# Table operands in PSUM, and all squares of x summed on TensorE, in an S5 block kernel

## The chip, the cores and the metric

One core of a Trainium2 chip runs the whole block; the other cores are idle. The metric is the device time of one execution in microseconds (us), over whole runs of the kernel. The core has five engines that run at the same time, each its own list of instructions in the order written: TensorE (PE in the rows; its loads of the stationary operand are PEld), VectorE (DVE), ScalarE (ACT), GpSimd (POOL), and SyncE (SP), which here only issues transfers. They wait for each other on semaphores. Matrix products and transposes are TensorE's and land in PSUM (8 banks of 512 numbers in each of 128 partitions); the rest of the data lies in SBUF.

## The reference

One layer of a diffusion block on 1024 latent tokens of width 1024, with 256 context tokens before them. Cut to what the change touches:

```python
mod = silu(c) @ ada_w + ada_b            # 6 x 1024; the context has its own, from c_ctx
xn  = modulate(rmsnorm(x, norm1_g), sh1, sc1)      # h * (1 + scale) + shift
cn  = modulate(rmsnorm(ctx, norm1_g), csh1, csc1)
for d in (forward, backward):            # S5: 64 groups of 16 channels, 64 complex states each
    lam_bar = exp(lam * dt);  k = (lam_bar - 1) / lam
    bb_re = k_re * b_re - k_im * b_im    # B_bar
    bb_im = k_re * b_im + k_im * b_re
    h_t = lam_bar * h_{t-1} + bb @ u_t   # context first, then the latent tokens
    y  += c_re @ h_re - c_im @ h_im
x = x + g1 * glu(gelu(y + d_skip * xn))
x = x + g2 * mlp(modulate(rmsnorm(x, norm2_g), sh2, sc2))     # 1024 -> 4096 -> 1024
out = rmsnorm(x, final_g)
```

All of it is float32.

## The kernel before

The program is written in issue order: each engine carries out its instructions in the order in which the Python text issues them, and no scheduler moves them. The tokens lie as 8 chunks `xu(j)`, 128 channels by 8 x 160 numbers (16 columns of context and 64 latent ones, for each of two halves). The scan is carried out in steps of 8 tokens: a table E of B_bar times powers of lam_bar turns 8 tokens at once into one state, so that TensorE can do it. The stages, in order of time:

- **Squares** (lines 148 to 154 and 171 to 197). ScalarE squares each chunk into one of four buffers (`sqt`, chosen by `sqb`), and TensorE sums over channels with a table `sel` into PSUM bank 1, eight matmuls a chunk. Of the first four chunks GpSimd adds 0 to 1 and 2 to 3 (L174, 128x1280), so that TensorE sums six buffers.
- **Discretisation** on VectorE (L158 to L207), then `b_bar` (L219 to L226) for groups 20 to 63 and later 0 to 19. ScalarE copies the powers into the tables `pt` (L193, L194) and, behind the last squares, `pg` (L209, L210). `transitions` (L256 to L261) fills tables that VectorE keeps in PSUM, and adds `pg[2]`.
- **Products of the tables** (`e_products`, L280 to L284): five instructions of 128x512 for each half chunk `(j, hlf)`, on VectorE for the five in `DVE_E`, on GpSimd for the other eleven. Both keep their inputs and the scratch operand `t` in SBUF. `turn_e` turns a half chunk with eight transposes and ScalarE copies the result (L296). Between them stand the scale of the tokens (L314 to L326) and the modulation: its matmuls (`cond1`, L301), the vector `md` (L429, L430), its spreading (L433) and ScalarE's copy `mu` (L437).
- **States and updates.** For every chunk j and group g `states` runs matmuls (L488 to L490) and two ScalarE copies (L491, L492). VectorE then runs `ups(j)`, five pieces of four instructions (L466 to L469) with their temporaries in PSUM; woven into its last piece is the context modulation `mod_ctx(j + 2)` (L450), two instructions of 128x256. `mod_ctx(0)` and `mod_ctx(1)` stand ahead of all updates. After chunks 5, 6 and 7 `k_finish` (L578 to L581) finishes a table of short kernels, which SyncE writes to memory in eight transfers (L584); on the same queue lie the writes of the modulated chunks (`save_u`, L453). GpSimd meanwhile makes the readout tables.
- **The scan** (L699 to L703) on VectorE, about 210 to 261 us, with five more `k_finish`; then readout, GLU gate and norm, and from about 475 us an MLP with a Strassen-like scheme (its matmuls are L772 to L774).

The lines that decide how the table products read their operands:

```python
eng, tm = (V, at(UT, 0, 5, 512)) if (j, hlf) in DVE_E else (P, sb(ETM, 5, 512))
er, ei, t = (vw(tm[:, i], 4, 16, 8) for i in (2 * hlf, 2 * hlf + 1, 4))
pr, pi, ps_ = (v[:, gs, None].to_broadcast(sh) for v in pt)
```

`at(UT, ...)` and `sb(...)` are SBUF, `bank(i)` and `PS` are PSUM; `vw` only gives a shape.

Of the kernel before, what the change touches and what calls it, by code (L numbers as in the profile page):

```python
# [10 lines left out]
OP = mybir.AluOpType  # L11
# [36 lines left out]
def kernel(ctx, tc, cst, bc, x, xl, ada_w, glu_w, w1, w2, out):  # L48
# [66 lines left out]
    ETM = 8192  # L115
# [26 lines left out]
    exb = C("ex")[:, None, :].to_broadcast([128, 64, NPOW])  # L142
    ssq = bank(1, 160)
    sqt = [at(E2[5], 0, 1280), at(E2[6], 0, 1280), at(E2[7], 0, 1280), at(X0, 2048, 1280)]
    sqb = (0, 1, 2, 3, 1, 3, 0, 2)

    def squares(j):
        S.activation(sqt[sqb[j]], xu(j, 1280), AF.Square)
# [19 lines left out]
    V.scalar_tensor_tensor(kk, ang, -1.0, ang, op0=OP.mult, op1=OP.max)  # L168
    S.activation(tb, ang, AF.Sin)
    S.activation(kk, kk, AF.Sin, scale=-1.0, bias=hpi)  # L170
    for j in (0, 2):
        squares(j)
        squares(j + 1)
        P.tensor_tensor(sqt[sqb[j]], sqt[sqb[j]], sqt[sqb[j + 1]], op=OP.add)  # L174
        sum_squares(j)
    V.tensor_scalar(sc, sc, 1.0, None, op0=OP.add)
    V.reciprocal(sc, sc)
# [17 lines left out]
    for j in range(4, 8):  # L195
        squares(j)
        sum_squares(j)

    V.tensor_scalar(q[0], pwr[:, :, 1], 1.0, None, op0=OP.subtract)
    V.tensor_tensor(q[3], pwi[:, :, 1], aim, op=OP.mult)  # L200
    V.tensor_tensor(q[2], q[0], are, op=OP.mult)
    V.tensor_tensor(q[4], pwi[:, :, 1], are, op=OP.mult)
    V.tensor_tensor(q[2], q[2], q[3], op=OP.add)
    V.tensor_tensor(q[3], q[0], aim, op=OP.mult)
    V.tensor_tensor(q[2], q[2], q[1], op=OP.mult)
    V.tensor_tensor(q[4], q[4], q[3], op=OP.subtract)
# [6 lines left out]
    def b_bar(a, b):  # L213

        gs = slice(a, b)
        n = b - a
        kre, kim = (q[i][:, gs, None].to_broadcast([128, n, 16]) for i in (2, 3))
        t1, t2 = (at(E2[4], 704 * i, n, 16) for i in range(2))
        V.tensor_tensor(t1, br[:, gs], kre, op=OP.mult)  # L219
        V.tensor_tensor(t2, bi[:, gs], kim, op=OP.mult)  # L220
        V.tensor_tensor(bd_[:, gs], bi[:, gs], kre, op=OP.mult)
        V.tensor_tensor(bi[:, gs], br[:, gs], kim, op=OP.mult)
        V.tensor_tensor(br[:, gs], t1, t2, op=OP.subtract)
        V.tensor_tensor(bi[:, gs], bi[:, gs], bd_[:, gs], op=OP.add)
# [27 lines left out]
    def transitions():  # L252

        for n in range(2):
            li = pwi[:, :, 8 + n]
            V.tensor_copy(LR[n], pwr[:, :, 8 + n])  # L256
            V.tensor_scalar(LI[n][:, :, 0], li, -1.0, None, op0=OP.mult)
            V.tensor_copy(LI[n][:, :, 1], li)
        V.tensor_copy(L32R, pwr[:, :, 10])
        V.tensor_copy(L32I, pwi[:, :, 10])  # L260
        V.tensor_tensor(pg[2], pg[0], pg[1], op=OP.add)  # L261

    def scan_transitions():
        l32 = L32.rearrange("p a g k c -> p (a g) k c")
# [65 lines left out]
    def dve_products(j, hlf):  # L330
        tp[j, hlf] = e_products(j, hlf)
# [1241 lines left out]
```

## Time and profile before

| | |
|---|---|
| time, median of 3 runs | 1100.47 us (1100.07 to 1103.93) |
| time of the profiled execution | 1100.8 us |
| its span, first to last instruction | 1099.0 us |
| mean granted clock of TensorE | 0.938 of full speed |
| busy: TensorE matmuls | 949.3 us (86%) |
| busy: VectorE | 915.3 us (83%) |
| busy: GpSimd | 610.4 us (56%) |
| busy: ScalarE | 551.3 us (50%) |
| chain that ended last | TensorE 46%, VectorE 31%, ScalarE 7%, issue 7%, DMA 4%, GpSimd 3% |

The chain is followed back from the last instruction to what released it, or to the instruction before it on its engine. Shares over the whole span mix stages with different limits, so a stage is read by its own window. In the rows, `out<-in` names the buffers: T and UT are the tables in SBUF, X the tokens and states, E the turned tables (and the buffers of the squares), GX a scratch tensor, PS is PSUM, KD and DX lie in memory. What stands in brackets at a row's end is the time that the engine was idle before the instruction, and the instruction that ended it. L12 is line 12 of the kernel before; in the orders below, of the changed kernel, lines of the later part are 4 to 11 higher.

### The profile page before, as it was taken

Reading aid. Unit: us, or ns where it says so; the run is one execution under the profiler, and the core shown is the slowest. Engines: PE = TensorE matmul, PEld = TensorE weight load, DVE = VectorE, ACT = ScalarE, POOL = GpSimd, SP = SyncE. Lnnn points to the kernel's source line nnn. Section 1 sums busy time; section 2 is a strip of 40 time slices with the busy share of each in tenths; the row PEclk is TensorE's granted clock in tenths of the full one; section 3 lists DMA queues with packets and bytes.
Section 4 is the critical chain, followed back from the end, with each engine's and each line's share of the span. In section 5 each row is a group of like instructions: output and inputs, shape, how many; then the busy total and the mean of one; then the engine's idle time right before and its main releaser. Section 6 shows DMA issues by size and latency. Waiting matters only on the chain.

```text
span 1099.0 us, 15197 instructions
## 1 busy us (share of the span) xinstructions
PE 949.3 (86%) x5244; PEld 779.7 (71%) x5244; DVE 915.3 (83%) x1393; ACT 551.3 (50%) x1012; POOL 610.4 (56%) x413
## 2 busy tenths in 40 slices
PE   3578675656799989789999999998889999999995
PEld 3347565535688867568888888886668888888875
DVE  8998999899993687789756565664899999999997
ACT  6238465334885446755655645453453434343413
POOL 3778899907373452354232324232788787778703
PEclk9779888776899999999999999999999999999998
DMA  9414355487576701145454444449453545351204
GB/s 385 181 31 147 118 163 139 96 220 202 164 234 210 254 20 38 68 158 191 162 175 139 157 149 156 161 139 339 165 190 131 174 135 164 123 193 39 77 1 154
DMA packets 104781, 168.85 MB, mean 154 GB/s; under 512 B 7680, under 2 KB 61952, under 8 KB 103424
## 3 DMA queue, kind: packets, MB, share of 16 engines
q1 hardware_dynamic: 100272, 153.20, 42.4%
q10 hardware_dynamic: 4432, 14.68, 4.1%
q8 instruction: 41, 0.67, 0.2%
q14 instruction: 36, 0.29, 0.1%
HBM read 120.40 MB, written 47.45 MB: 153 GB/s over the span
## 4 chain that ended last, share of the span: by engine, by line
PE 46%; DVE 31%; ACT 7%; issue 7%; DMA 4%; POOL 3%; SPq 1%; DVEq 0%; POOLq 0%; ACTq 0%
PE PS L774 14%; PE PS L773 14%; PE PS L772 14%; DVE T L1353 3%; DVE X L469 2%; DVE X L468 2%; DMA DY<-X 2%; DVE PS L467 2%; DVE PS L466 2%; DVE z L923 1%; DVE PS L699 1%; DVE W L923 1%; ACT T L724 1%; DVE X L450 1%; DVE UT L701 1%
## 5 line engine op out<-in xcount | busy, mean ns | idle before, releaser
L772 PE MATMUL PS<-z,W 128*128 128x512 f32 (+1 forms) x432 | 168.7, 390 | 2.9 <-DVE T L1173 1.5
L773 PE MATMUL PS<-z,W 128*128 128x512 f32 (+1 forms) x432 | 168.0, 389 | 2.4 <-DVE z L923 2.4
L774 PE MATMUL PS<-z,W 128*128 128x512 f32 (+1 forms) x404 | 156.9, 388 | 1.3 <-POOL W L923 1.2
L1353 DVE SCALAR_TENSOR_TENSOR T<-PS,T 128x512 f32<-128x512 f32 x160 | 112.1, 739 | 2.4 <-PE PS L774 2.2
L773 PE MATMUL PS<-W 128*128 128x512 f32 (+1 forms) x244 | 94.5, 387 | 4.7 <-DVE W L923 4.7
L772 PEld LDWEIGHTS PS<-z,W 128*128 128x128 f32 x432 | 81.8, 189 | 20.7 <-DVE T L1452 2.2
L773 PEld LDWEIGHTS PS<-z,W 128*128 128x128 f32 x432 | 81.8, 189 | 19.9 <-DVE z L923 3.7
L772 PE MATMUL PS<-W 128*128 128x512 f32 (+1 forms) x244 | 93.9, 385 | 0.0
L774 PEld LDWEIGHTS PS<-z,W 128*128 128x128 f32 x404 | 76.6, 190 | 18.1 <-POOL W L923 2.1
L923 DVE TENSOR_TENSOR z<-z 128x512 fp32r<-128x512 f32 x60 | 81.2, 1378 | 6.0 <-ACT z L926 6.0
L774 PE MATMUL PS<-W 128*128 128x512 f32 (+1 forms) x216 | 83.4, 386 | 1.5 <-POOL W L923 1.5
L774 PE MATMUL PS<-z,A 128*128 128x512 f32 x208 | 81.3, 391 | 2.5 <-POOL A L923 2.5
L923 DVE TENSOR_TENSOR W<-W 128x512 fp32r<-128x512 f32 x49 | 74.1, 1535 | 7.2 <-ACT W L926 7.2
L1201 POOL TENSOR_TENSOR T<-T 128x512 f32<-128x512 f32 x27 | 39.2, 1455 | 68.2 <-ACT T L1144 60.0
L488 PE MATMUL PS<-X,E 128*64 128x160 f32 x256 | 50.4, 337 | 29.0 <-DVE X L450 17.1
L774 PE MATMUL PS<-W,A 128*128 128x512 f32 x184 | 71.7, 390 | 0.3 <-POOL A L923 0.3
L772 PE MATMUL PS<-z,A 128*128 128x512 f32 x180 | 70.2, 390 | 0.0
L1173 DVE TENSOR_TENSOR T<-T,PS 128x512 f32<-128x512 f32 x64 | 42.9, 684 | 32.7 <-PE PS L774 32.0
L773 PE MATMUL PS<-z,A 128*128 128x512 f32 x180 | 70.0, 389 | 0.0
L926 ACT CAST W<-T 128x512 fp32r<-128x512 f32 (+1 forms) x46 | 33.0, 718 | 65.1 <-POOL T L1272 42.5
L926 ACT CAST W<-UT 128x512 fp32r<-128x512 f32 (+2 forms) x50 | 35.6, 713 | 58.6 <-POOL UT L1272 37.8
L488 PEld LDWEIGHTS PS<-X,E 128*64 128x64 f32 x256 | 34.8, 152 | 40.2 <-issue 22.9
(329 smaller groups left out, 2780.8 us busy)
## 6 DMA issues: line engine op xcount, KB each, us to landing
YD<-T SPq DMA_DIRECT2D x88, 256.0 KB, 2.3
z<-YD SPq DMA_DIRECT2D x60, 256.0 KB, 3.8
W<-YD SPq DMA_DIRECT2D x49, 256.0 KB, 4.1
T<-in_w_dram SPq DMA_DIRECT2D x9, 1024.0 KB, 5.8
T<-in_ada_w_dram ACTq DMA_DIRECT2D x17, 512.0 KB, 4.1
UT<-in_w_dram SPq DMA_DIRECT2D x8, 1024.0 KB, 5.8
T<-in_w_dram SPq DMA_DIRECT2D x20, 384.0 KB, 3.4
UT<-in_w_dram SPq DMA_DIRECT2D x15, 384.0 KB, 4.4
```

The costliest lines, as they stand in the source:

```text
L466: ops = [lambda: eng.tensor_tensor(ta, src, lr, op=OP.mult), lambda: eng.tensor_tensor(tb_, src[:, :, ::-1], li, op=OP.mult), lambda: eng. ...
L467: lambda: eng.tensor_tensor(tb_, src[:, :, ::-1], li, op=OP.mult),
L468: lambda: eng.tensor_tensor(out_, out_, ta, op=OP.add),
L488: PE.matmul(b[0:64, c], e[:, g, c, 0:64], uj[:, g], start=True, stop=True)
L772: PE.matmul(o, wt[0], xt[0], start=start, stop=False)
L773: PE.matmul(o, wt[0], xt[1], start=False, stop=False)
L774: PE.matmul(o, wt[1], xt[0], start=False, stop=stop)
L923: eng.tensor_tensor(lo, src, hi.bitcast(F32), op=OP.subtract)
L926: S.copy(vw(to[0][:, 0:size(dims)], *dims) if dims else to[0], src)
L1173: V.tensor_tensor(to, x_, o, op=OP.add)
L1201: P.tensor_tensor(o, x_, z_, op=op)
L1353: V.scalar_tensor_tensor(o, src, g2[:, d:d + 1], o, op0=OP.mult, op1=OP.add)
```

## The change

It has five parts.

1. ScalarE's squares of all eight chunks go to TensorE one by one; GpSimd's two adds are gone, and the square buffers rotate in plain order.
2. Powers of the first 20 groups (`pt[0]` and `pt[1]`, all that VectorE's products need) are copied to PSUM bank 1 (`ptv`, two ScalarE copies), behind the sums of squares that lie in the same bank. VectorE's products read them there and keep their scratch `t` in PSUM too.
3. The factors k of the discretisation (`hold`) and two temporaries of `b_bar` (`t2`, `t3`) lie in PSUM.
4. The sum `pg[2]` moves from ahead of VectorE's first product to behind its third.
5. The context's modulation of chunks 2 to 7 is copied to PSUM (`muc`, one ScalarE copy) and read there by `mod_ctx`; `k_finish` on VectorE keeps the two values `dj` and `ks` in PSUM.

```diff
-    sqb = (0, 1, 2, 3, 1, 3, 0, 2)
+    sqb = (0, 1, 2, 3, 0, 1, 2, 3)
...
-    for j in (0, 2):
+    for j in range(4):
         squares(j)
-        squares(j + 1)
-        P.tensor_tensor(sqt[sqb[j]], sqt[sqb[j]], sqt[sqb[j + 1]], op=OP.add)
         sum_squares(j)
...
+    ptv = [vw(bank(1, 160, 160 + 160 * i), 20, 8) for i in range(2)]
+    for i in range(2):
+        S.copy(ptv[i], pt[i][:, 0:20])
+
+    hold = [PS[:, 3616 + 64 * i:3680 + 64 * i] for i in range(2)]
...
-    V.tensor_tensor(q[2], q[2], q[1], op=OP.mult)
+    V.tensor_tensor(hold[0], q[2], q[1], op=OP.mult)
     V.tensor_tensor(q[4], q[4], q[3], op=OP.subtract)
-    V.tensor_tensor(q[3], q[4], q[1], op=OP.mult)
+    V.tensor_tensor(hold[1], q[4], q[1], op=OP.mult)
...
-        t1, t2 = (at(E2[4], 704 * i, n, 16) for i in range(2))
+        kre, kim = (h[:, gs, None].to_broadcast([128, n, 16]) for h in hold)
+        t1, t2, t3 = at(E2[4], 0, n, 16), *(vw(PS[:, o:o + 16 * n], n, 16) for o in (1024, 2048))
         V.tensor_tensor(t1, br[:, gs], kre, op=OP.mult)
         V.tensor_tensor(t2, bi[:, gs], kim, op=OP.mult)
-        V.tensor_tensor(bd_[:, gs], bi[:, gs], kre, op=OP.mult)
+        V.tensor_tensor(t3, bi[:, gs], kre, op=OP.mult)
...
-        V.tensor_tensor(bi[:, gs], bi[:, gs], bd_[:, gs], op=OP.add)
+        V.tensor_tensor(bi[:, gs], bi[:, gs], t3, op=OP.add)
...
-        V.tensor_tensor(pg[2], pg[0], pg[1], op=OP.add)
...
-        er, ei, t = (vw(tm[:, i], 4, 16, 8) for i in (2 * hlf, 2 * hlf + 1, 4))
+        er, ei = (vw(tm[:, i], 4, 16, 8) for i in (2 * hlf, 2 * hlf + 1))
+        t = vw(PS[:, 2976:3488] if on_v else tm[:, 4], 4, 16, 8)
...
-        pr, pi, ps_ = (v[:, gs, None].to_broadcast(sh) for v in pt)
+        pr, pi, ps_ = (v[:, gs, None].to_broadcast(sh) for v in (*(ptv if on_v else pt[:2]), pt[2]))
...
     dve_products(1, 0)
+    V.tensor_tensor(pg[2], pg[0], pg[1], op=OP.add)
...
+    muc = vw(PS[:, 3488:3584], 8, 2, 6)
     S.copy(mu, vw(bank(6, 256), 8, 2, 8, 2))
+    S.copy(muc, mu[:, :, :, 2:8, 1])
...
-        sc_, sh_ = (mu[:, :, i, j, 1:2][:, :, :, None].to_broadcast([128, 8, 2, 16]) for i in (1, 0))
+        sc_, sh_ = ((mu[:, :, i, j, 1:2] if j < 2 else muc[:, :, i, j - 2:j - 1])[:, :, :, None].to_broadcast([128, 8, 2, 16]) for i in (1, 0))
...
+            dj, ks = (vw(PS[r:r + 16, o:o + 128], 8, 16) for o in (3200, 3328))
...
-        eng.tensor_tensor(kf, kf, dj, op=OP.add)
-        eng.tensor_tensor(k0, k0, kf, op=OP.add)
+        eng.tensor_tensor(ks, kf, dj, op=OP.add)
+        eng.tensor_tensor(k0, k0, ks, op=OP.add)
```

ScalarE before, from the fifth square (L148) over the four `pg` copies (L209, L210) to the root for the token scale (L315):

```order
L148 ACTIVATE E_6_76<-X_69 128x1280 [waits DMAHW6_49,Pool_49]
L148 ACTIVATE X_68<-X_69 128x1280 [waits DMAHW7_49,Pool_49]
L148 ACTIVATE E_5_75<-X_69 128x1280 [waits DMAHW0_49,PE_49]
L148 ACTIVATE E_7_77<-X_69 128x1280 [waits DMAHW1_49,PE_49]
L209 COPY T<-E_2_72 64x512
L210 COPY T<-E_2_72 64x512
L209 COPY T<-UT 64x512
L210 COPY T<-UT 64x512
L315 ACT_TABLE_LOAD
L315 ACTIVATE GX<-GX 128x160 [waits DVE_49]
```

The same stretch now (the `pg` copies are L212 and L213, the root is L319):

```order
L148 ACTIVATE E_5_75<-X_69 128x1280 [waits DMAHW6_49,PE_49,Activation_49]
L148 ACTIVATE E_6_76<-X_69 128x1280 [waits DMAHW7_49,PE_49,Activation_49]
L148 ACTIVATE E_7_77<-X_69 128x1280 [waits DMAHW0_49,PE_49,Activation_49]
L148 ACTIVATE X_68<-X_69 128x1280 [waits DMAHW1_49,PE_49,Activation_49]
L199 COPY PS<-T 128x160 [waits PE_49,Activation_49]
L199 COPY PS<-T 128x160 [waits Activation_49]
L212 COPY T<-E_2_72 64x512
L213 COPY T<-E_2_72 64x512
L212 COPY T<-UT 64x512
L213 COPY T<-UT 64x512
L319 ACT_TABLE_LOAD
L319 ACTIVATE GX<-GX 128x160 [waits DVE_49]
```

Two copies from T to PSUM (L199) stand between the last square and the `pg` copies, and the first of them waits for TensorE.

VectorE before, from the last table copy to PSUM (L260) over the sum `pg[2]` (L261) and the products of (0,0) (L280 to L284) to the first row of the token scale:

```order
L260 COPY PS<-UT 128x64 [waits DVE_49]
L261 TENSOR_TENSOR T<-T 128x512 [waits Activation_49]
L280 TENSOR_TENSOR UT<-T 128x512 [waits DVE_49,Pool_49]
L281 TENSOR_TENSOR UT<-T 128x512
L282 TENSOR_TENSOR UT<-UT 128x512 [waits DVE_49]
L283 TENSOR_TENSOR UT<-T 128x512 [waits DVE_49]
L284 TENSOR_TENSOR UT<-UT 128x512 [waits DVE_49]
L314 TENSOR_SCALAR GX<-PS 128x160 [waits PE_49]
```

The same place now (products L284 to L288):

```order
L263 COPY PS<-UT 128x64 [waits DVE_49]
L284 TENSOR_TENSOR UT<-T 128x512 [waits DVE_49,Activation_49,Pool_49]
L285 TENSOR_TENSOR PS<-PS,T 128x512 [waits PE_49]
L286 TENSOR_TENSOR UT<-UT,PS 128x512 [waits DVE_49]
L287 TENSOR_TENSOR PS<-PS,T 128x512 [waits DVE_49]
L288 TENSOR_TENSOR UT<-UT,PS 128x512 [waits DVE_49]
L318 TENSOR_SCALAR GX<-PS 128x160
```

The sum is gone from here, the first product also waits for ScalarE, the second for TensorE, and four of the five have a PSUM input.

VectorE before, the products of (2,0) and the first context modulation (L450):

```order
L280 TENSOR_TENSOR UT<-T 128x512
L281 TENSOR_TENSOR UT<-T 128x512
L282 TENSOR_TENSOR UT<-UT 128x512 [waits DVE_49]
L283 TENSOR_TENSOR UT<-T 128x512 [waits DVE_49]
L284 TENSOR_TENSOR UT<-UT 128x512 [waits DVE_49]
L450 TENSOR_TENSOR X_69<-X_69,T 128x16x16 [waits Activation_49]
```

The same place now, from the product's first row:

```order
L284 TENSOR_TENSOR UT<-T 128x512
L285 TENSOR_TENSOR PS<-PS,T 128x512 [waits DVE_49,PE_49,Activation_49]
L286 TENSOR_TENSOR UT<-UT,PS 128x512 [waits DVE_49]
L287 TENSOR_TENSOR PS<-PS,T 128x512 [waits DVE_49]
L288 TENSOR_TENSOR UT<-UT,PS 128x512 [waits DVE_49]
L457 TENSOR_TENSOR X_69<-X_69,T 128x16x16
```

The second product has taken over the wait for ScalarE, and waits for TensorE as well.

## Rows read from the trace of the kernel before

**Rows 1.** VectorE's waits, 0 to 261 us: us in total, times, longest us.
```profile
DVE PS L466 <- ACT X L491: 4.1, 2, 2.1
DVE T L429 <- PE PS L424: 0.7, 1, 0.7
```

**Rows 2.** Timeline of GpSimd and VectorE: start us, us, then the instruction.
```profile
15.14 2.95 POOL L174 TENSOR_TENSOR E<-E,E 128x1280 f32<-128x1280 f32 x1 [10.40 <-ACT E L148]
15.24 2.94 DVE L200 TENSOR_TENSOR UT<-UT,T 128x64 f32<-128x64 f32 x1
```

**Rows 3.** VectorE's timeline, 69 and 262 us; updates by shape (busy us, mean ns).
```profile
69.04 0.68 DVE L280 TENSOR_TENSOR UT<-T 128x512 f32<-128x512 f32 x1
L466 DVE TENSOR_TENSOR PS<-X,PS 128x528 f32<-128x528 f32 x24 | 17.0, 710 | 5.0 <-ACT X L491 4.1
262.61 0.69 DVE L466 TENSOR_TENSOR UT<-X,PS 128x512 f32<-128x512 f32 x1
```

**Rows 4.** TensorE's timeline, sums: matmuls, then weight loads (18 to 19.5 us).
```profile
18.15 9.46 PE L154 MATMUL PS<-E,T 128*128 128x160 f32 x48 [18.15 <-POOL E L174]
29.61 4.51 PE L154 MATMUL PS<-E,T 128*128 128x160 f32 x32
18.15 1.57 PEld L154 LDWEIGHTS PS<-E,T 128*128 128x128 f32 x6 [18.15 <-POOL E L174]
```

**Rows 5.** ScalarE's timeline: the first three squares, the first `pg` copy.
```profile
12.65 3.57 ACT L148 ACTIVATE E<-X 128x1280 f32<-128x1280 f32 x3
26.65 0.62 ACT L209 COPY T<-E 64x512 f32<-64x512 f32 x1
```

**Rows 6.** VectorE's timeline: where products (0,0), (1,0), (2,0) begin and end.
```profile
42.19 1.74 DVE L280 TENSOR_TENSOR UT<-T 128x512 f32<-128x512 f32 x1
49.94 0.31 DVE L314 TENSOR_SCALAR GX<-PS 128x160 f32<-128x160 f32 x1
58.45 1.59 DVE L280 TENSOR_TENSOR UT<-T 128x512 f32<-128x512 f32 x1
66.24 2.87 DVE L326 TENSOR_TENSOR X<-X,PS 128x1280 f32<-128x1280 f32 x2
76.32 1.53 DVE L280 TENSOR_TENSOR UT<-T 128x512 f32<-128x512 f32 x1
81.61 1.62 DVE L450 TENSOR_TENSOR X<-X,T 128x256 f32<-128x256 f32 x2
```

**Rows 7.** Timelines of ScalarE and VectorE: modulation copy, VectorE's second update.
```profile
80.01 0.38 ACT L437 COPY T<-PS 128x256 f32<-128x256 f32 x1 [2.67 <-PE PS L433]
94.56 0.71 DVE L466 TENSOR_TENSOR PS<-X,PS 128x528 f32<-128x528 f32 x1 [2.01 <-ACT X L491]
```

**Rows 8.** VectorE: context modulation by shape; a 128x256 update on the timeline.
```profile
L450 DVE TENSOR_TENSOR X<-X,T 128x256 f32<-128x256 f32 x16 | 17.2, 1076 | 0.1
275.12 0.41 DVE L466 TENSOR_TENSOR UT<-X,PS 128x256 f32<-128x256 f32 x1
```

**Rows 9.** Timelines of VectorE and ScalarE: `k_finish` and what stands around it.
```profile
175.12 1.24 DVE L578 TENSOR_TENSOR T<-T 16x128 f32<-16x128 f32 x1
178.88 0.71 DVE L466 TENSOR_TENSOR PS<-X,PS 128x528 f32<-128x528 f32 x1
207.02 0.67 DVE L578 TENSOR_TENSOR T<-T 16x128 f32<-16x128 f32 x1
210.10 0.28 DVE L265 COPY PS<-PS 128x128 f32<-128x128 f32 x1
228.04 0.28 DVE L580 TENSOR_TENSOR T<-T 16x128 f32<-16x128 f32 x1
189.71 0.38 ACT L491 COPY X<-PS 128x264 f32<-128x264 f32 x1 [10.98 <-DMA DX<-X]
197.53 0.71 DVE L466 TENSOR_TENSOR PS<-X,PS 128x528 f32<-128x528 f32 x1 [2.07 <-ACT X L491]
```

**Rows 10.** Windows: us, each engine's busy us (count), PEclk, DMA share, GB/s.
```profile
475.00:1089.00 614.00, 596.56 (x2654) 489.50 (x2652) 501.14 (x640) 281.47 (x454) 327.50 (x189) 1.00 0.45 150
```

More of the change, by code (lines that the diff above doesn't have):

```diff
@@ L216, in b_bar @@
         n = b - a
-        kre, kim = (q[i][:, gs, None].to_broadcast([128, n, 16]) for i in (2, 3))
-        t1, t2 = (at(E2[4], 704 * i, n, 16) for i in range(2))
+        kre, kim = (h[:, gs, None].to_broadcast([128, n, 16]) for h in hold)
+        t1, t2, t3 = at(E2[4], 0, n, 16), *(vw(PS[:, o:o + 16 * n], n, 16) for o in (1024, 2048))
         V.tensor_tensor(t1, br[:, gs], kre, op=OP.mult)
         V.tensor_tensor(t2, bi[:, gs], kim, op=OP.mult)
-        V.tensor_tensor(bd_[:, gs], bi[:, gs], kre, op=OP.mult)
+        V.tensor_tensor(t3, bi[:, gs], kre, op=OP.mult)
         V.tensor_tensor(bi[:, gs], br[:, gs], kim, op=OP.mult)
         V.tensor_tensor(br[:, gs], t1, t2, op=OP.subtract)
-        V.tensor_tensor(bi[:, gs], bi[:, gs], bd_[:, gs], op=OP.add)
+        V.tensor_tensor(bi[:, gs], bi[:, gs], t3, op=OP.add)
         V.tensor_tensor(bs[:, gs], br[:, gs], bi[:, gs], op=OP.add)
@@ L272, in e_products @@
     def e_products(j, hlf):
-        eng, tm = (V, at(UT, 0, 5, 512)) if (j, hlf) in DVE_E else (P, sb(ETM, 5, 512))
-        er, ei, t = (vw(tm[:, i], 4, 16, 8) for i in (2 * hlf, 2 * hlf + 1, 4))
+        on_v = (j, hlf) in DVE_E
+        eng, tm = (V, at(UT, 0, 4, 512)) if on_v else (P, sb(ETM, 5, 512))
+        er, ei = (vw(tm[:, i], 4, 16, 8) for i in (2 * hlf, 2 * hlf + 1))
+        t = vw(PS[:, 2976:3488] if on_v else tm[:, 4], 4, 16, 8)
         gs = slice(8 * j + 4 * hlf, 8 * j + 4 * hlf + 4)
         sh = [128, 4, 16, 8]
-        pr, pi, ps_ = (v[:, gs, None].to_broadcast(sh) for v in pt)
+        pr, pi, ps_ = (v[:, gs, None].to_broadcast(sh) for v in (*(ptv if on_v else pt[:2]), pt[2]))
         b, d, s = (v[:, gs, :, None].to_broadcast(sh) for v in (br, bd_, bs))
@@ L577, in k_finish @@
         k0, kf, dj = ksr(j, 0, 8, 15, 16)[:, :, 7], ksr(j, 1920, 8, 16), ksr(j, 2048, 8, 16)
+        ks = kf
+        if eng is V:
+            r = 32 + 64 * (j % 2)
+            dj, ks = (vw(PS[r:r + 16, o:o + 128], 8, 16) for o in (3200, 3328))
         eng.tensor_tensor(dj, ident[32:48, None, 32:48].to_broadcast([16, 8, 16]),
                         C("dg")[32:48, 8 * j:8 * j + 8, None].to_broadcast([16, 8, 16]), op=OP.mult)
-        eng.tensor_tensor(kf, kf, dj, op=OP.add)
-        eng.tensor_tensor(k0, k0, kf, op=OP.add)
+        eng.tensor_tensor(ks, kf, dj, op=OP.add)
+        eng.tensor_tensor(k0, k0, ks, op=OP.add)
         kd = KD[j].rearrange("(h t g c) -> t h g c", h=16, t=8, g=8)
```

## The prediction

> **What bounds the kernel now.** I read the page's busy slices first, then the chain of work that ended last, then VectorE's waits up to the scan's end, the timeline of the four engines that the change touches, and the windows by stage.
>
> VectorE's waits over the first 261 us are short: ScalarE's copies of the states hold it 4.1 us, TensorE 0.7 us [rows 1]. Up to the end of the scan VectorE is therefore the spine of the program, and every microsecond taken from its instructions, or from something it comes to wait for, moves all that follows. After it come the readout, the gate and the MLP, which the change does not touch, and which should slide as a block; the MLP's 614 us are TensorE's, 596.6 us busy at a granted clock of 1.00 [rows 10].
>
> Why VectorE is slow in places is seen in two stretches. While GpSimd runs its 128x1280 add for 2.95 us, a VectorE product of 64 elements a row takes 2.94 us: it starts 0.1 us later and ends together with it [rows 2]. The instructions of the table products, 128x512 with both inputs in SBUF, take 0.68 us where GpSimd is idle [rows 3] and 1.5 to 1.7 us where it runs its own products [rows 6]. The update instruction with one input in PSUM is not held: 24 of 128x528 average 710 ns though GpSimd works through most of that stage [rows 3]. So the reading is that an instruction with two SBUF inputs waits for the GpSimd instruction in progress, and one with a PSUM input does not.
>
> **The change, part by part.** The sum is made against the profiled execution, 1100.8 us (span 1099.0), which is 0.3 us above the median of the three runs.
>
> *The gate of the first product.* Part (0,0) starts at 42.19 us now [rows 6]. Without GpSimd's two adds VectorE loses two holds of nearly 3 us each, without the sum `pg[2]` 0.6 us, and so could be there at about 36.1; the PSUM temporaries of `b_bar` make it earlier still (its last eight instructions run beside GpSimd). But the first product now waits for ScalarE's last `pg` copy, these stand behind the two new table copies, and those wait for the last sum of squares. That sum is longer: 64 matmuls instead of 48, of two records each. The 96 records now run from 18.15 to 34.12 us, 2.4 us more than 96 at the later pace of 0.141 us (4.51 us for 32), because the first ones ran at 0.26 (1.57 us for six) [rows 4]. With the first square done at 13.9 [rows 5] I take 13.95 + 128 x 0.141 + 2.4 = 34.4 for the last sum. All at the fast pace it is 32.0, all at the slow pace 47.2. Two table copies of 128x160, priced at no more than ScalarE's 0.38 us for 128x256 [rows 7], and four `pg` copies of 0.62 [rows 5], with the hand-overs, give a start at **38.0: 4.2 us gained**. All else gained before that point goes into VectorE's new wait. Behind it on VectorE stands everything; GpSimd's own products, which take no part in that wait, start earlier.
>
> *The five products.* Two of the five instructions of each keep two SBUF inputs only in the first (`ei`); four get a PSUM input. One held instruction at 1.35 us (between 0.6 and 1.7) and four at 0.7 us give 4.1. Now (0,0) takes 7.75 us, (1,0) 7.79, (2,0) 5.29, and (1,1), undisturbed, 5 x 0.68 = 3.4 [rows 3, 6]. That gains 3.65 in (0,0) and 3.7 in (1,0), and loses 0.5 in (1,1), if GpSimd is then at work; (0,1), held in its first instruction alone, stays as it is. The moved `pg[2]` sum costs up to 1.3 where it now stands (0.64 alone, more beside GpSimd). VectorE's 0.7 us wait for the modulation's transposes goes [rows 1], since TensorE's chain there was itself late by (1,0). In (2,0) the second instruction now waits for the modulation matmuls and two ScalarE copies, because its PSUM bank is one that TensorE's sums of modulation fill: about 0.6 lost in all. With the gate this is 4.2 + 3.65 + 3.7 - 0.5 - 1.3 + 0.7 - 0.6 = 9.85 us at the first context modulation (81.6 now [rows 6]).
>
> VectorE then waits 2.01 us at its second update for ScalarE's state copies [rows 7]. These hang on the modulation copy at 80.01, whose matmuls come earlier by 10.45 (all of that but the last 0.6) and no longer stand behind a pair of transposes; the new 128x96 copy takes back under 0.38. The update should resume 11.2 us earlier, between VectorE's 9.85 and some 11.6 of the copies. **First part: 11.2** (bounds 7 to 14).
>
> *Context modulation.* Sixteen instructions of 128x256 with two SBUF inputs average 1.076 us; twelve of them, for chunks 2 to 7, get a PSUM input. VectorE's 128x256 with one PSUM input takes 0.41 us [rows 8]. 12 x (1.076 - 0.41) = **8.0 us**, all on VectorE, in the stage where it hardly waits. The lower bound is nothing, if the state copies cannot come faster.
>
> *Finishing the short kernels.* `k_finish(0)` takes from 175.12 to 178.88, `k_finish(2)` from 207.02 to 210.10, each three instructions of 128 elements; undisturbed ones in the scan take 0.28 [rows 9]. The first still has two SBUF inputs and stays, the other two get a PSUM input: 1.24 + 2 x 0.28 = 1.8, and 0.67 + 0.56 = 1.2. Gain 2.0 + 1.9 = **3.8 us** (0 to 4.5). `k_finish(1)` is given nothing, since VectorE waits 2.07 us for ScalarE soon behind it [rows 9]: ScalarE's copies before that stand 10.98 us for a saved chunk, which lies on SyncE's queue behind the eight writes of `k_finish(0)`. Those in the scan gain nothing either.
>
> *Free edits.* The factors `hold` in PSUM and `b_bar`'s temporaries lie ahead of the gate, under VectorE's new wait; without the gate they would be worth some 4 us more. SyncE's and GpSimd's queues carry the same transfers in the same order.
>
> Sum: 11.2 + 8.0 + 3.8 = 23.0; 1100.8 - 23.0 = **1077.8, forecast 1078 us**.
>
> [...] An update writing a 128x512 buffer in SBUF from one SBUF and one PSUM input takes 0.69 us, the same work from two SBUF inputs 0.68 [rows 3]: moving an operand costs an undisturbed instruction 0.01 us at most, and the sum counts nothing. [...]
>
> **The rivals.**
>
> *TensorE stays slow through the sums.* Then the last sum ends at 47.2 and the gate opens 12.8 us later: 1077.8 + 12.8 = **1090.6**. For it: the first records ran at 0.26 [rows 4]. Against: the rest ran at 0.141 without a break, and the new sums are denser. Chance 0.08.
>
> *The state copies bound the updates.* VectorE gets through its modulation sooner and waits for ScalarE or TensorE as long: 1077.8 + 8.0 = **1085.8**. For it: two waits of 2 us there now [rows 1]. Against: there are no others of that size in that stage. Chance 0.12.
>
> *The change does not do what it says:* an instruction with one SBUF input is held by GpSimd all the same. Products, modulation and `k_finish` stay as they are, and the gate's 4.2 with the lost wait of 0.7, less 1.3 for `pg[2]`, is all: 1100.8 - 3.6 = **1097**. Against: the 710 ns of 24 updates [rows 3]. Chance 0.03.
>
> [...] Chance 0.05. [...]
>
> *Slower: TensorE gets a lower clock in the MLP.* The 614 us there ran at 1.00 [rows 10]; a kernel that reaches them sooner, with other pauses before, may get less. Each 0.01 costs some 6 us, so 0.04 eats the gain and below about 0.954 the kernel is slower by over 0.5%: 1077.8 + 614 x 0.05 = **1108**. Nothing in the trace speaks for it beyond the clock having been below 1.00 in earlier stages. Chance 0.03.
>
> **How the numbers follow.** The forecast has 0.69, the rivals 0.08, 0.12, 0.03, 0.05 and 0.03. The forecast's own bounds (first part 7 to 14, `k_finish` 0 to 4.5) give 1074 to 1086 around 1078; taking in the second and fourth rival and leaving out the others the range is **1073 to 1088**. About 0.5%, 5.5 us, is what a measurement of this kernel tells from no change. Faster by more than that: all but the third and the last, 0.93 (with a share for surprises taken off); same 0.04, slower 0.03.
>
> **What would show it.** In the changed kernel: GpSimd free of the 128x1280 adds, and VectorE's products of 64 elements back at about 0.2 us; VectorE waiting some 4 to 8 us for ScalarE before the first product, which starts near 38; four of five product instructions at 0.7 us beside a busy GpSimd; twelve modulations near 0.41; the scan starting near 187 instead of 210; the MLP at clock 1.00 over 614 us. The forecast is wrong if the first product starts after 42, if VectorE's waits for ScalarE between 80 and 190 grow by more than 5 us, or if the stage after the scan grows, because its loads from memory come no sooner.

## The result

The changed kernel takes 1075.3 us at the median of 4 runs (1074.2 to 1078.0), against 1102.2 us (1100.1 to 1105.6) for the kernel before in the same comparison: a ratio of 0.9757, 95% interval 0.9737 to 0.9777. In a second comparison it took 1076.2 against 1102.6 us, 0.9768 (0.9743 to 0.9792). The forecast was 1078, range 1073 to 1088. The two profiled executions stand 26.0 us apart, with spans of 1099.0 and 1073.0 us.

| | before | after |
|---|---|---|
| profiled execution, us | 1100.8 | 1074.8 |
| span, us | 1099.0 | 1073.0 |
| mean granted clock of TensorE | 0.938 | 0.944 |
| busy: TensorE matmuls, us | 949.3 | 954.5 |
| busy: VectorE, us | 915.3 | 884.0 |
| busy: GpSimd, us | 610.4 | 599.7 |
| busy: ScalarE, us | 551.3 | 552.9 |

VectorE lost 31.3 us of busy time and TensorE gained 5.2, of which 4.2 are in the sums that GpSimd no longer shortens. VectorE's waits up to 261 us, which before were those of [rows 1], one of 0.5 us, and one of 4.0 us at the very start (now 3.8), are now these (us in total, times, longest us):

```profile
DVE UT L284 <- ACT T L213: 5.6, 1, 5.6
DVE PS L473 <- ACT X L498: 3.8, 2, 2.7
...
DVE PS L285 <- ACT PS L444: 1.4, 1, 1.4
```

The first and the last are the two waits that the change puts in, in the places where the prediction had them. The first is the gate of the first product. TensorE's timeline and ScalarE's show what it hangs on: the last sum ends at 31.41 + 2.34 = 33.75 us, and the two table copies (L199) and four `pg` copies (L212, L213) follow at once.

```profile
13.79 9.09 PE L154 MATMUL PS<-E,T 128*128 128x160 f32 x48 [13.79 <-ACT E L148]
...
24.89 6.68 PE L154 MATMUL PS<-E,T 128*128 128x160 f32 x48
31.41 2.34 PE L154 MATMUL PS<-X,T 128*128 128x160 f32 x16
```

```profile
33.84 0.62 ACT L199 COPY PS<-T 128x160 f32<-128x160 f32 x2 [7.43 <-PE PS L154]
34.40 0.64 ACT L212 COPY T<-E 64x512 f32<-64x512 f32 x1
...
36.38 0.67 ACT L213 COPY T<-UT 64x512 f32<-64x512 f32 x1
```

VectorE's timeline from the gate on, with the two waits, the first context modulation and the second update:

```profile
15.07 0.26 DVE L203 TENSOR_TENSOR UT<-UT,T 128x64 f32<-128x64 f32 x1
...
37.13 1.17 DVE L284 TENSOR_TENSOR UT<-T 128x512 f32<-128x512 f32 x1 [5.61 <-ACT T L213]
38.22 0.69 DVE L285 TENSOR_TENSOR PS<-PS,T 128x512 f32<-128x512 f32 x1
...
68.43 0.70 DVE L285 TENSOR_TENSOR PS<-PS,T 128x512 f32<-128x512 f32 x1 [1.42 <-ACT PS L444]
...
71.23 2.08 DVE L457 TENSOR_TENSOR X<-X,T 128x256 f32<-128x256 f32 x2
...
83.99 0.71 DVE L473 TENSOR_TENSOR PS<-X,PS 128x528 f32<-128x528 f32 x1 [1.11 <-ACT X L498]
```

The row at 15.07 is the 64-element product that took 2.94 us beside GpSimd's add [rows 2] and now takes 0.26. The product (0,0) begins at 37.13 and is over in 3.9 us instead of 7.75 [rows 6]: its first instruction, still with two SBUF inputs, takes 1.17 us, the second, which reads PSUM, 0.69. The modulation of 128x256 by shape (busy us, mean ns) stands at 0.41 us, the price of [rows 8]:

```profile
L457 DVE TENSOR_TENSOR X<-X,PS 128x256 f32<-128x256 f32 x12 | 5.0, 413 | 0.0
```

And the finish of the short kernels after chunk 5, with the update that follows it, and VectorE's wait after the next one, answering to [rows 9]:

```profile
155.12 0.82 DVE L589 TENSOR_TENSOR PS<-T 16x128 f32<-16x128 f32 x1
156.04 0.29 DVE L591 TENSOR_TENSOR PS<-T,PS 16x128 f32<-16x128 f32 x1
156.43 0.28 DVE L592 TENSOR_TENSOR T<-T,PS 16x128 f32<-16x128 f32 x1
156.74 0.71 DVE L473 TENSOR_TENSOR PS<-X,PS 128x528 f32<-128x528 f32 x1
...
175.01 0.71 DVE L473 TENSOR_TENSOR PS<-X,PS 128x528 f32<-128x528 f32 x1 [2.71 <-ACT X L498]
```

Where the 26.0 us came from is read by the start of the same instruction in both traces:

| | before, us | after, us | gained up to here |
|---|---|---|---|
| first product, VectorE | 42.19 | 37.13 | 5.1 |
| first context modulation | 81.61 | 71.23 | 10.4 |
| second update | 94.56 | 83.99 | 10.6 |
| finish after chunk 5 | 175.12 | 155.12 | 20.0 |
| first instruction of the scan | 210.9 | 186.5 | 24.4 |
| behind the scan | 260.70 | 237.06 | 23.6 |
| first matmul of L774 with operand W, MLP | 477.2 | 452.7 | 24.5 |
| first of VectorE's sums L1353, MLP | 775.0 | 748.9 | 26.1 |
| end | 1099.0 | 1073.0 | 26.0 |

All but 1.6 us was won by the scan's first instruction. The scan itself gave 0.8 us back, the stretch between it and the MLP won 0.9, and the MLP added 1.6.

### The profile page after: what moved, and what is told of

Read it like the earlier page. It is cut to its first block, busy times and chain, and to the rows that moved or that the text cites. A ratio compares the mean times of both kernels' runs of the same rounds, so it can differ in the third digit from the quotient of the medians.

```text
span 1073.0 us, 15268 instructions
## 1 busy us (share of the span) xinstructions
PE 954.5 (89%) x5276; PEld 783.5 (73%) x5276; DVE 884.0 (82%) x1393; ACT 552.9 (52%) x1015; POOL 599.7 (56%) x411
## 4 chain that ended last, share of the span: by engine, by line
PE 54%; DVE 24%; ACT 8%; issue 5%; POOL 4%; DMA 4%; SPq 1%; DVEq 0%; ACTq 0%; POOLq 0%
PE PS L784 15%; PE PS L785 15%; PE PS L783 15%; DVE T L1364 3%; DVE X L476 2%; PE PS L154 2%; DVE X L475 2%; DMA DY<-X 1%; DVE z L934 1%; DVE PS L474 1%; DVE PS L473 1%; DVE W L934 1%; DVE PS L710 1%; PE PS L573 1%; PE PS L495 1%
## 5 line engine op out<-in xcount | busy, mean ns | idle before, releaser
L785 PE MATMUL PS<-W,A 128*128 128x512 f32 x184 | 71.7, 390 | 0.3 <-POOL A L934 0.3
L783 PE MATMUL PS<-W,A 128*128 128x512 f32 x156 | 60.7, 389 | 0.0
```

Source lines behind the costliest of these rows:

```text
L783: PE.matmul(o, wt[0], xt[0], start=start, stop=False)
L785: PE.matmul(o, wt[1], xt[0], start=False, stop=stop)
```

## The experiments

Eleven kernels were run, each timed against the kernel before. Below, "the change" is the changed kernel of these runs at 1076.2 us. Seven of the others are the change with one part taken back or put elsewhere. They were timed in three comparisons, whose kernels before took 1102.6 to 1102.7 us; a difference between two runs is that of their medians.

**The yardstick.** No edit.

> The changed kernel once more, as the yardstick of these runs. Every theory expects about 1075 us, and VectorE's first product at 37 us behind a wait of some 5.6 us for ScalarE.

Measured: 1076.2 us, 0.9768 (0.9743 to 0.9792). The first product begins at 37.81 us behind a wait of 6.1 us. This trace lacks the wait at the product (2,0), and the scan begins at 187.95 us instead of 186.54: two executions of one kernel differ by 1.4 us there.

**The context modulation, taken out and put in alone.** Taken out of the change:

```diff
-    S.copy(muc, mu[:, :, :, 2:8, 1])
...
-        sc_, sh_ = ((mu[:, :, i, j, 1:2] if j < 2 else muc[:, :, i, j - 2:j - 1])[:, :, :, None].to_broadcast([128, 8, 2, 16]) for i in (1, 0))
+        sc_, sh_ = (mu[:, :, i, j, 1:2][:, :, :, None].to_broadcast([128, 8, 2, 16]) for i in (1, 0))
```

> The change with all context modulation read from SBUF again (no copy to PSUM). Theory (VectorE is the spine of the update stage, and an instruction with two SBUF inputs waits for GpSimd's): twelve instructions go from 0.41 to about 1.08 us, 8.0 us, some 9 with what follows; 1083 to 1085 us. Rival (ScalarE's state copies pace the updates): within 2 us of the change, VectorE's waits for ScalarE being that much shorter.

Measured: 1086.7 us, 0.9867 (0.9843 to 0.9891), which is 10.6 us more than the change. The reverse was run too, the same lines added to the kernel before and nothing else:

> The kernel before with one part of the change alone: the context modulation of chunks 2 to 7 read from PSUM. Theory (this part is worth its own time, whatever the others do): twelve instructions from 1.16 us each (13.96 us for the twelve, the other four of the sixteen taking 3.24) to 0.41, 9.0 us, less 0.3 for the ScalarE copy ahead of the states: 0.992 of the kernel before, some 1093.5 us. Rival (ScalarE's copies pace the updates when VectorE gets faster): under 4 us.

Measured: 1094.5 us against 1102.7, 0.9924 (0.9905 to 0.9942): 8.2 us. The groups by shape of the first and of the second (busy us, mean ns):

```profile
L455 DVE TENSOR_TENSOR X<-X,T 128x256 f32<-128x256 f32 x16 | 18.5, 1156 | 0.1
```

```profile
L452 DVE TENSOR_TENSOR X<-X,PS 128x256 f32<-128x256 f32 x12 | 5.0, 413 | 0.0
...
L452 DVE TENSOR_TENSOR X<-X,T 128x256 f32<-128x256 f32 x4 | 4.4, 1094 | 0.1
```

Both ways the part is worth about its own time, 8 to 11 us, as the theory had it. In the traces the scan begins 8.5 us earlier with this part alone (202.46 against 210.95), and without it 9.9 us later than in the change (196.44), 8.5 later than in the yardstick; 1.5 us more came in the MLP of that trace (last section). The kernel with this part alone reaches its second update 2.6 us later than the kernel before (97.13 against 94.56), held more often ahead of it, and wins 11 us from there to the scan. ScalarE's copies do not take it back: VectorE's wait at its update lines for them is 3.3 us in the kernel with this part alone, 4.0 us in the change without it and 3.8 in the change.

**The finish of the short kernels in SBUF.**

```diff
-        if eng is V:
-            r = 32 + 64 * (j % 2)
-            dj, ks = (vw(PS[r:r + 16, o:o + 128], 8, 16) for o in (3200, 3328))
```

> The change with the two values of the short-kernel finish in SBUF again. Theory: the finish after chunk 5 takes 3.8 us again instead of 1.6 and the one after chunk 7 3.1 instead of 1.2, the one after chunk 6 is taken up by VectorE's wait for ScalarE's copies; 4 us in all, 1079 us. Rival (SyncE's writes and ScalarE's copies behind them set the pace): within 1 us of the change.

Measured: 1080.2 us, 0.9803 (0.9787 to 0.9820), 4.0 us more than the change. The one after chunk 6 is the instructive one. Its place in this run, with the wait that follows:

```profile
169.91 0.28 DVE L586 TENSOR_TENSOR T<-T 16x128 f32<-16x128 f32 x1
170.23 1.24 DVE L588 TENSOR_TENSOR T<-T 16x128 f32<-16x128 f32 x1
171.51 1.11 DVE L589 TENSOR_TENSOR T<-T 16x128 f32<-16x128 f32 x1
...
176.04 0.71 DVE L473 TENSOR_TENSOR PS<-X,PS 128x528 f32<-128x528 f32 x1 [1.14 <-ACT X L498]
```

Its three instructions take 2.7 us here instead of 1.4, and the wait behind them is 1.14 us instead of the 2.71 of the change: what the one gains the other gives back, nearly as the sum had it. From the finish after chunk 5 to the scan's first instruction this trace takes 34.2 us, the change's 31.4 and the yardstick's 32.3; the MLP adds 1.5 us to this trace, of the kind that the last section shows.

**The factors and temporaries of `b_bar` in SBUF.**

```diff
-    hold = [PS[:, 3616 + 64 * i:3680 + 64 * i] for i in range(2)]
+    hold = [q[2], q[3]]
...
-        t1, t2, t3 = at(E2[4], 0, n, 16), *(vw(PS[:, o:o + 16 * n], n, 16) for o in (1024, 2048))
+        t1, t2, t3 = at(E2[4], 0, n, 16), at(E2[4], 704, n, 16), bd_[:, gs]
```

> The change with the factors k and the temporaries of b_bar in SBUF again. Theory (this part lies under VectorE's wait for ScalarE's pg copies): the last eight b_bar instructions go from about 0.45 to 1.35 us, VectorE comes 5 us later to a gate at which it waited 5.6 us; the time stays within 1 us of the change, and the wait shrinks to under 1 us. Rival (each held instruction that is freed counts): 1080 us.

Measured: 1077.1 us, 0.9777 (0.9747 to 0.9806), the change within its interval. VectorE's timeline, at the second `b_bar` instruction of the first 20 groups and at the gate:

```profile
24.54 1.36 DVE L223 TENSOR_TENSOR E<-T,UT 128x320 f32<-128x320 f32 x1
...
36.52 1.61 DVE L284 TENSOR_TENSOR UT<-T 128x512 f32<-128x512 f32 x1 [0.34 <-ACT T L213]
```

The `b_bar` instructions are held again, VectorE comes 4.7 us later, and the wait of 5.6 us is down to 0.34. This part of the change is worth nothing beside the gate.

**GpSimd's adds back.**

```diff
-    for j in range(4):
+    for j in (0, 2):
         squares(j)
+        squares(j + 1)
+        P.tensor_tensor(sqt[sqb[j]], sqt[sqb[j]], sqt[sqb[j + 1]], op=OP.add)
         sum_squares(j)
```

(with the order of the square buffers of the kernel before.)

> The change with GpSimd's two adds back and six sums on TensorE instead of eight. Theory (the last sum ends at 34 us with either, and the gate hangs on it): VectorE is held twice, 5.4 us in all, and arrives at about 37, the gate opens at about 37.5; time within 1 us of the change, so this part of it is worth next to nothing. Rival (the two holds of nearly 3 us were on the path, and their removal is a large part of the gain): 1080 us.

Measured: 1076.7 us, 0.9778 (0.9752 to 0.9803), again the change within its interval. VectorE's and TensorE's timelines:

```profile
15.30 2.93 DVE L205 TENSOR_TENSOR UT<-UT,T 128x64 f32<-128x64 f32 x1
18.16 2.93 DVE L206 TENSOR_TENSOR UT<-UT,T 128x64 f32<-128x64 f32 x1
...
37.88 0.84 DVE L286 TENSOR_TENSOR UT<-T 128x512 f32<-128x512 f32 x1 [0.68 <-ACT T L215]
```

```profile
30.01 4.51 PE L154 MATMUL PS<-E,T 128*128 128x160 f32 x32
```

VectorE is held twice, 2.93 us each time, and the last sum ends at 34.5 instead of 33.75 us: the first product begins at 37.88, where it begins without the adds (37.13 and 37.81). So the two holds, the most striking rows of the profile before, were worth nothing to the change as it stands: the sums that replace the adds take as long.

**The table copies by VectorE, and the gate gone.**

```diff
-    ptv = [vw(bank(1, 160, 160 + 160 * i), 20, 8) for i in range(2)]
-    for i in range(2):
-        S.copy(ptv[i], pt[i][:, 0:20])
+    ptv = [vw(PS[:, 2432 + 160 * i:2592 + 160 * i], 20, 8) for i in range(2)]
...
     transitions()
+    for i in range(2):
+        V.tensor_copy(ptv[i], pt[i][:, 0:20])
```

> The change with the two table copies made by VectorE, into a bank that TensorE does not use, ahead of its first product, instead of by ScalarE behind the sums. Theory (VectorE waits 5.6 us at a gate that hangs on the last sum of squares): the pg copies are then done near 29, VectorE starts its first product at 32.1 instead of 37.1, 0.6 us of copies counted; 5 us less, 1070.3 us. Rival (the token scale, the modulation's matmuls or their weights from memory come next): within 1.5 us of the change, with a new wait of VectorE for TensorE before 70 us.

Measured: 1071.6 us, 0.9721 (0.9700 to 0.9742), 4.5 us less than the change. The edit changes two things, the engine that copies and the bank that it writes; a run that changes one of them alone was not made. The first product begins at 32.19 us without a wait, and the second update 6 us earlier than in the change, though with a longer wait for ScalarE. The scan begins at 181.52 us, 5.0 earlier; in the MLP this trace gives 2.4 us back (last section).

```profile
32.19 1.01 DVE L282 TENSOR_TENSOR UT<-T 128x512 f32<-128x512 f32 x1
...
78.04 0.71 DVE L473 TENSOR_TENSOR PS<-X,PS 128x528 f32<-128x528 f32 x1 [2.41 <-ACT X L498]
```

**The same, and all context modulation from PSUM.** In addition to the edit above:

```diff
+    muf = vw(PS[:, 3744:3776], 8, 2, 2)
+    S.copy(muf, mu[:, :, :, 0:2, 1])
...
-        sc_, sh_ = ((mu[:, :, i, j, 1:2] if j < 2 else muc[:, :, i, j - 2:j - 1])[:, :, :, None].to_broadcast([128, 8, 2, 16]) for i in (1, 0))
+        sc_, sh_ = ((muf[:, :, i, j:j + 1] if j < 2 else muc[:, :, i, j - 2:j - 1])[:, :, :, None].to_broadcast([128, 8, 2, 16]) for i in (1, 0))
```

> The table copies by VectorE as in the run before, and the context modulation of chunks 0 and 1 read from PSUM as well (one more ScalarE copy of 128x32). Theory: 5 us from the gate and 4 x (0.99 - 0.41) = 2.3 us from these four instructions, less 0.2 us for the copy ahead of the states: 1068 us. Rival (ScalarE's state copies hold the second update, so that the last 2 us turn into waiting): 1070 us.

Measured: 1070.7 us, 0.9719 (0.9701 to 0.9736): the rival. The four instructions take 0.87 us a pair, and the second update begins at 78.75 us, no earlier than the 78.04 of the run before.

**ScalarE's modulation of chunk 1 behind the states of chunk 0.** In addition to both edits above:

```diff
-            for g_ in [g] if j < 6 else range(2 * g, 2 * g + 2) if j == 6 and g < 4 else []:
+            for g_ in (range(8) if g == 7 else []) if j == 0 else [g] if j < 6 else range(2 * g, 2 * g + 2) if j == 6 and g < 4 else []:
```

> The version with the table copies by VectorE and all modulation of the context from PSUM, and ScalarE's modulation of the latent tokens of chunk 1 moved behind all state copies of chunk 0 instead of between them. Theory (the 2 us that this version did not win are VectorE's wait of 2.41 us at its second update for ScalarE's state copies, which the interleaved modulation delays): that wait shrinks to under 0.8 us and the time falls by 2 us to some 1068.5. Rival (the states of chunk 1 then come as much later, or TensorE paces the state copies anyway): within 1 us of 1070.7, with a wait of VectorE of 2 us at the second update or the one after.

Measured: 1070.4 us, 0.9708 (0.9693 to 0.9723): the rival again. VectorE's second update, and ScalarE's copy of the fifth group of chunk 0 (L500), which stands idle for TensorE:

```profile
78.20 0.71 DVE L475 TENSOR_TENSOR PS<-X,PS 128x528 f32<-128x528 f32 x1 [2.81 <-ACT X L500]
```

```profile
74.54 0.38 ACT L500 COPY X<-PS 128x264 f32<-128x264 f32 x1 [1.26 <-PE PS L499]
```

With its modulation out of the way ScalarE waits for TensorE's states instead, and VectorE's wait is 2.81 us where it was 2.41. This run is the lowest ratio of the study, and the three versions without the gate lie within each other's intervals, all below the change.

**What a held instruction costs: the scratch in SBUF, then the powers.** First only the scratch operand was put back:

```diff
-        eng, tm = (V, at(UT, 0, 4, 512)) if on_v else (P, sb(ETM, 5, 512))
+        eng, tm = (V, at(UT, 0, 5, 512)) if on_v else (P, sb(ETM, 5, 512))
...
-        t = vw(PS[:, 2976:3488] if on_v else tm[:, 4], 4, 16, 8)
+        t = vw(tm[:, 4], 4, 16, 8)
```

> The change with the scratch operand of VectorE's products in SBUF again, the powers staying in PSUM. Theory (it is the second SBUF input that is held): the third and fifth instruction of each product have two SBUF inputs and go from 0.7 to 1.3 to 1.6 us wherever GpSimd runs, the second and fourth stay at 0.7 although they now write SBUF; about 0.7 us each for six to ten of them, less 1.4 us for the wait at the product (2,0), which goes: 3 to 5 us more, 1078 to 1080 us. Rival (writing SBUF is held too): four instructions of each product slow, 1083 us or more.

Measured: 1075.7 us, 0.9764 (0.9747 to 0.9781). Both were wrong: no time was lost. The product (1,0), and the second update:

```profile
50.04 1.59 DVE L284 TENSOR_TENSOR UT<-T 128x512 f32<-128x512 f32 x1
51.55 0.68 DVE L285 TENSOR_TENSOR UT<-PS,T 128x512 f32<-128x512 f32 x1
52.27 1.03 DVE L286 TENSOR_TENSOR UT<-UT 128x512 f32<-128x512 f32 x1
53.34 0.69 DVE L287 TENSOR_TENSOR UT<-PS,T 128x512 f32<-128x512 f32 x1
54.06 0.71 DVE L288 TENSOR_TENSOR UT<-UT 128x512 f32<-128x512 f32 x1
...
84.03 0.71 DVE L473 TENSOR_TENSOR PS<-X,PS 128x528 f32<-128x528 f32 x1 [2.33 <-ACT X L498]
```

The first instruction is held for the full price, but the third and fifth, which have two SBUF inputs too, take 1.03 and 0.71 us. Each stands behind an instruction that was not held. The first four products lose 1.7 us in all against the change, the fifth wins back 2.5, since without a scratch in PSUM it does not wait for the modulation's copies and was not held, and the second update begins at 84.03, as in the change (83.99), for it waits for ScalarE. That gave the theory of the next run, in which the powers lie in SBUF and the scratch in PSUM, so that the held instructions are the first, second and fourth:

```diff
-    ptv = [vw(bank(1, 160, 160 + 160 * i), 20, 8) for i in range(2)]
-    for i in range(2):
-        S.copy(ptv[i], pt[i][:, 0:20])
...
-        pr, pi, ps_ = (v[:, gs, None].to_broadcast(sh) for v in (*(ptv if on_v else pt[:2]), pt[2]))
+        pr, pi, ps_ = (v[:, gs, None].to_broadcast(sh) for v in pt)
```

> The change with the powers read from SBUF again by VectorE's products (no table copies), the scratch operand staying in PSUM. The run with the scratch in SBUF showed third and fifth instructions of 0.7 to 1.05 us where 1.3 to 1.6 had been expected. Theory (a held instruction waits for the rest of the GpSimd instruction in progress, so it costs little behind an instruction that was not held, and much behind one that was): in the first and third product the second instruction takes about 1.5 us, coming behind the held first one, the fourth about 0.85 to 1.05, the third and fifth 0.7; the gate opens at 32 instead of 37 us. Rival (a held instruction costs the same wherever it stands): second and fourth alike. On the whole the gate gives 5 us and the products take some 4 back, and the second update waits for ScalarE: 1073 to 1076 us by either.

Measured: 1076.5 us, 0.9767 (0.9748 to 0.9787). The product (1,0) again, and GpSimd's instructions beside it:

```profile
45.87 1.55 DVE L281 TENSOR_TENSOR UT<-T 128x512 f32<-128x512 f32 x1
47.34 1.75 DVE L282 TENSOR_TENSOR PS<-T 128x512 f32<-128x512 f32 x1
49.13 0.69 DVE L283 TENSOR_TENSOR UT<-UT,PS 128x512 f32<-128x512 f32 x1
49.85 0.72 DVE L284 TENSOR_TENSOR PS<-T 128x512 f32<-128x512 f32 x1
50.60 0.69 DVE L285 TENSOR_TENSOR UT<-UT,PS 128x512 f32<-128x512 f32 x1
```

```profile
45.73 1.14 POOL L282 TENSOR_TENSOR T<-T 128x512 f32<-128x512 f32 x1
46.95 1.59 POOL L283 TENSOR_TENSOR T<-T 128x512 f32<-128x512 f32 x1
48.62 1.39 POOL L284 TENSOR_TENSOR T<-T 128x512 f32<-128x512 f32 x1
```

The second instruction, behind a held one, takes 1.75 us, the fourth, behind a free one, 0.72: the theory, and not the rival, by which the two would be alike. The held instruction at 47.34 ends at 49.09, 0.55 us behind the end of GpSimd's instruction that began at 46.95 (48.54); the one at 45.87 and the one at 49.85 end 0.55 and 0.56 us behind GpSimd's too (46.87 and 50.01). In the other products the second took 1.76, 1.56 and 1.56 us where it stood behind a held one, the fourth 0.72 to 1.25. So a held instruction waits for the rest of GpSimd's current one: two in a row alternate with GpSimd's and pay nearly all of it, one behind 0.7 us of free work pays little. GpSimd pays as well, 1.59 us for an instruction that takes 1.26 undisturbed (at 61.26).

Together the two runs take back each operand of the products by itself; none takes back both, so what reading them from PSUM is worth in all is read from the rows of the result, not from a run.

## Why the prediction was right

The forecast of 1078 us lies 2.7 us above the measured 1075.3, inside the range, and its steps can be held against the trace one by one. The sum had 23.0 us, the traces show 26.0: 0.6 less than forecast in the first part, 1.4 more in the context modulation, 0.6 more in the finish, and 1.6 behind the scan's start, which the sum did not have.

- **The gate.** Put at 38.0 with the last sum at 34.4; it was 37.13 with 33.75. The two copies ahead of `pg` took 0.56 us together instead of 0.76. What the prediction had hidden there (the adds of GpSimd, the temporaries of `b_bar`) is hidden: two runs that take these parts back stay at 1076.7 and 1077.1 us, and the run without the gate shows the price of the gate, 4.5 us. That `b_bar`'s part would be worth some 4 us without the gate was not tried.
- **The products.** Put at 4.1 us each; (0,0) took 3.9, (0,1) 3.7, (1,0) 4.3, (1,1) 4.2. The held first instructions took 1.02 to 1.69 where 1.35 was taken. By its own numbers the sum should have taken 0.7 off for (1,1) and not 0.5; it was 0.8. The price of a hold was read from rows in which one held instruction follows another, and that is where it holds; the two runs on the products show that it doesn't elsewhere. The forecast did not hang on it, since the change leaves no such case in the products but the first instruction.
- **First context modulation and second update.** 9.85 and 11.2 us earlier were forecast, 10.4 and 10.6 measured. The first came so near partly by luck. Two small VectorE instructions that the sum did not have, L324 and L435, fell beside GpSimd's and took 1.09 and 0.56 us instead of 0.49 and 0.18 (L320 and L430 before), which with the larger loss in (1,1) is 1.3 us; 0.9 more at the gate and 0.5 in (0,1), which was to stay as it was, made up for it. In the second the chain was wrong. The state copies were to hang on the modulation copy, and this came 12.3 us earlier (67.72 against 80.01), but the state copies only 10.6:

```profile
67.72 0.38 ACT L443 COPY T<-PS 128x256 f32<-128x256 f32 x1 [3.03 <-PE PS L438]
73.46 0.50 PE L495 MATMUL PS<-X,E 128*64 128x160 f32 x1 [0.34 <-DVE X L457]
74.99 0.38 ACT L498 COPY X<-PS 128x264 f32<-128x264 f32 x1 [0.90 <-PE PS L497]
```

TensorE's states stand behind the turned product (2,0) and VectorE's first context modulation, and begin 10.0 us earlier than before (73.46 against 83.45). Their first 3.0 us run at a granted clock of 0.50, which before were 1.5 us, and ScalarE's first state copy waits 0.90 us for them. The sum had not followed that.
- **Context modulation of chunks 2 to 7: the term that was mis-sized.** 8.0 us were forecast; from the second update to the finish after chunk 5 the change gained 20.0 - 10.6 = 9.4. The mean of 1.076 us in [rows 8] is that of all sixteen instructions, and four of them, at 81.61 and 88.75, were the cheap ones, 3.24 us together: the twelve had 17.2 - 3.24 = 13.96, 1.16 us each, and 13.96 - 12 x 0.41 = 9.0. A mean over the group that the change doesn't touch whole hid 1 us; the instances by time would have shown it. A wait of half a microsecond in that stage went too.
- **The finish of the short kernels.** 3.8 us forecast, and 4.0 by the run that takes it back; 20.0 to 24.4 in the trace, 19.5 to 23.0 in the yardstick's. The first of the three stayed dear (0.82 and 0.50 us, with its two SBUF inputs), the others cost 0.3, and the finish after chunk 6 won 0.4, the rest of it going into the wait behind.
- **The slide of the rest.** The scan gave back 0.8 us, which the prediction did not have: VectorE reaches it 24.4 us earlier, while GpSimd's readout tables, which end at 208 instead of 221 us, come only 13 us earlier. GpSimd is thus busy 26.3 us beside the scan instead of 16.6, and the first two of VectorE's four finishes in it take 0.6 us longer: 1.15 and 0.50 us for their first instructions, which took 0.77 and 0.28. The 0.9 us between the scan and the MLP were not followed; the 1.6 us of the MLP came in its first 25 us, below.

Of the rivals the first (TensorE slow through the sums) did not come about: 48 records took 9.09 us at first, then 48 took 6.68, which is 0.139 each. The second (state copies bound the updates) holds at the second update and behind the finish after chunk 6 (waits of 1.11 and 2.71 us), and at the former it decides what the better versions can still win. The third is refuted by the rows of the products and of the modulation. The fourth, which has a chance of 0.05 and is taken into the range, is a price for reading PSUM, and no run shows such a price: a product instruction with an input in PSUM took 0.69 us at 38.22, against 0.68 from SBUF [rows 3], and an instruction of `b_bar` of 128x704 with GpSimd idle 0.88 us from SBUF before (at 23.06) and 0.89 with an input in PSUM now (at 17.50). The fifth, a lower clock in the MLP, did not come about: it is 1.00 from 450 to 974 us, as it was from 475 to 1000 us before, and 0.95 in the last 99 us of both.

## What to carry to other kernels

Where VectorE and GpSimd work side by side, look for VectorE instructions with two SBUF inputs that end together with a GpSimd instruction (2.94 us beside an add of 2.95 here, 0.26 without it), and move one operand of them to PSUM; what it wins is worth its time only in a stretch in which VectorE waits for nobody (8 to 11 us for the context modulation, 0.9, inside the interval, for `b_bar` ahead of the gate). A held instruction cost the rest of GpSimd's current one here (1.75 us behind a held one, 0.72 behind a free one), so of a run of them breaking every second is nearly as good as all (4.3 to 4.7 us for each of the first four products here, against 3.7 to 4.3; with none broken (0,0) and (1,0) took 7.8). And a copy into PSUM should not stand behind a sum that it does not need: here ScalarE's two copies went into the bank of the sums of squares and waited 7.43 us for the last of them, and the version in which VectorE makes them, into other banks, is 4.5 us faster. Whether the bank alone would have done it, with ScalarE copying, was not tried. The gate, not the freed instructions, decided the first 37 us.

## What the runs showed of the hardware

The clock granted to TensorE when the MLP begins differs between profiled executions of kernels that do the same there. The first 25 us of the MLP in three of them (windows: us, each engine's busy us (count), PEclk, DMA share, GB/s), before:

```profile
475.20:500.20 25.00, 21.78 (x87) 16.91 (x86) 21.47 (x28) 11.66 (x20) 12.87 (x9) 0.93 0.53 179
```

```profile
450.70:475.70 25.00, 21.78 (x93) 16.95 (x92) 19.91 (x27) 11.46 (x19) 12.24 (x9) 1.00 0.54 177
```

```profile
450.70:475.70 25.00, 22.46 (x84) 17.26 (x83) 20.41 (x27) 11.50 (x20) 12.39 (x9) 0.86 0.54 177
```

The granted clock is 0.93 in the kernel before, 1.00 after (second fence) and 0.86 with `b_bar` in SBUF (third). With the matmuls about equally busy, 87, 93 and 84 of them got done. TensorE's way to the first sums of L1353 is 297.8 us before (775.0 - 477.2), 296.2 after and 298.3 with `b_bar` in SBUF (751.0 - 452.7). In the version with all context modulation from PSUM the clock of these 25 us is 1.00 again, with 93 matmuls done, and the way 296.2 us (743.8 - 447.6), so in these four it goes with the clock. The yardstick's way is 296.2 us too (750.0 - 453.8); the longest read is 298.6 (747.4 - 448.8), in the version whose one edit has VectorE make the table copies. So up to 2.1 us between two of the four are not won or lost by the instructions that the edits touch, and the 1.6 us that the change gained in its MLP are of this kind. What the clock followed there was not tried, nor whether it stays the same from one execution of a kernel to the next, beyond the equal way of the two of the change.
